# Linear attention layer: head 0's gates and block products ahead of the samples' projection, the samples' state updates behind head 1

## The chip, the cores and the metric

The kernel runs on one core of a Trainium2 chip. The metric is the time of one execution on the device in microseconds, as the median of several runs. The profile is of one execution: its engines are PE (TensorE, matmuls; PEld is its weight load), DVE (VectorE), ACT (ScalarE), POOL (GpSimd) and SP (SyncE, which issues nearly all DMAs here).

## The reference

One inference step of a two-layer decoder: a gated linear attention (GLA) layer, then a differential-attention layer, each followed by an MLP, for one prompt of 16 meta tokens and 1024 tokens and for 8 running sequences ("samples") of one new token each. The change lies wholly in the GLA layer:

```python
def gla_project(x, w_in, w_gate, b_gate):
    h = x @ w_in
    q, k, v, r, g_low = jnp.split(h, [qk, 2 * qk, 2 * qk + vv, 2 * qk + 2 * vv], axis=-1)
    ...
    lg = jax.nn.log_sigmoid((g_low @ w_gate + b_gate).astype(F32)) / GLA_TAU

def gla_chunk(state, q, k, v, lg):
    b = jnp.cumsum(lg, axis=1)
    o_inter = jnp.einsum('blhd,bhde->blhe', q * jnp.exp(b), state)
    causal = jnp.tril(jnp.ones((L, L), bool))[None, :, :, None, None]
    diff = b[:, :, None] - b[:, None, :]
    decay = jnp.where(causal, jnp.exp(jnp.where(causal, diff, 0.0)), 0.0)
    scores = jnp.einsum('bihd,bjhd,bijhd->bhij', q, k, decay)
    o_intra = jnp.einsum('bhij,bjhe->bihe', scores, v)
    b_last = b[:, -1]
    new_state = jnp.exp(b_last)[..., None] * state + jnp.einsum(
        'blhd,blhe->bhde', k * jnp.exp(b_last[:, None] - b), v)
    return new_state, o_inter + o_intra

def gla_sample(x, state, w_in, w_gate, b_gate, g_norm, w_out):
    q, k, v, lg, r = gla_project(x, w_in, w_gate, b_gate)
    s_new, o = gla_chunk(state.astype(F32), q, k, v, lg)
    return gla_output(o, r, g_norm, w_out, x.dtype), s_new
```

There are 4 heads; a head's state is 128 x 256 floats, so one sample's state is 512 KB. The updated states of the samples (`gla_state_s`) and the prompt's final states (`gla_state_p`) are outputs.

## The kernel before

The kernel is one long function; a scheduler orders each engine's instructions by the order in which they are emitted and by its own estimate of when operands are ready. On the chip each engine then runs its list in that fixed order, and a waiting instruction holds up those behind it on its engine. Tiles come from pools; a tile waits until the former holder of its buffer has been read for the last time.

Two streams of work share the GLA layer.

The **prompt** goes head by head, h = 0 to 3. `proj(h, qk)` loads and splits a head's weights into a high and a low part (`unit`, `kunit`; two buffers `whi`/`wlo` each) and projects q and k (2 halves c of 512 tokens, 4 PSUM tiles of pool `mm`, which has 3 banks) and then v (4 more tiles, copied by ACT into `Yh[:, h]`, a part of the big tile Y; L323). Then, for each half c: the gate product (L631), the log gate (L383 to L388), four scans (L639), seven levels of decayed block products (`level`, L420 to L426, on DVE and ACT; L649, L664 on PE), qh (q with decay), kt (k with decay, transposed; L684). Then four steps, each over 128 tokens, advance the state (L692 to L696): three products, one DVE instruction for the new state, which the next step needs. After the four heads come the r gates (kunit, L718 to L727), and then the layer's output projection.

The **samples**, with the meta tokens as 32 rows together, go through the layer's projection (L351, L358), their own gates, their products with the 8 states (L483), their state updates (L484 to L487), the output projection, norm and MLP (L519, L573), and the second layer's projection (L590, L519). Their weights, 48 loads of 1 MB after the states, come through the pool `swt` of two buffers, in the order of emission. The emission of `proj(0)` is interleaved with the samples' projection by `next(first)`; the rest of head 0 and heads 1 to 3 is emitted behind the whole samples' path (L624 and following).

The samples' states pass through three slots in Y. Y holds 8192 columns, head h's v in columns 2048 h to 2048 h + 2047, so that the slots at 5120, 6144 and 7168 lie in the second half of head 2's v and in head 3's v. `sv`, the samples' v, lies in 4096 to 5119. Sample b's slot is loaded, used by the products of L483, multiplied and added to in place with a broadcast of `vs` (in a swt tile, `vbs`), stored, and loaded anew with sample b + 3.

Of the kernel before, what the change touches and what calls it, by code (L numbers as in the profile page):

```python
# [21 lines left out]
P = 128  # L22
# [3 lines left out]
NM = 16  # L26
# [85 lines left out]
def hybrid_step(ctx, tc, A, dbg=None, upto=9):  # L112
# [154 lines left out]
    dma(graw, wir[:, :, 3072:3088])  # L267
    for c in range(2):
# [65 lines left out]
    for c in range(2):  # L334
# [6 lines left out]
        V.tensor_tensor(go, go, ga, op=ALU.add)  # L341
    qk = {}
    first = proj(0, qk)
    next(first)
# [3 lines left out]
    for k in range(NB):  # L348
# [3 lines left out]
        if k % 2:  # L352
            next(first)
    for k in range(0, NB, 2):
# [21 lines left out]
    wg = gp.tile([48, 512], F32, name="wg")  # L376
    for c in range(2):
        dma(wg[32 * c : 32 * c + 16, :], A["gla_w_gate"][0])

    def log_gate(z, n, h):  # L380

        a = t2()[:, :n]
        S.activation(a, z, AF.Abs, bias=bg[:, h : h + 1])  # L383
        S.activation(a, a, AF.Exp, scale=-1.0)
        S.activation(a, a, AF.Ln, bias=1.0)
        m = t2()[:, :n]
        V.tensor_scalar(m, z, bg[:, h : h + 1], 0.0, ALU.add, ALU.min)
        V.tensor_tensor(m, m, a, op=ALU.subtract)  # L388
        return m

# [24 lines left out]
    def level(b, q, k, u, s, eng):  # L415

        sh = [P, b.shape[1] // (2 * s), 2 * s]
        bv = b.rearrange("p (n s) -> p n s", s=2 * s)
        uv = u.rearrange("p (n s) -> p n s", s=2 * s)
        V.tensor_tensor(uv, bv, bv[:, :, s - 1 : s].broadcast_to(sh), op=ALU.subtract)  # L420
        S.activation(uv[:, :, :s], uv[:, :, :s], AF.Exp, scale=-1.0 / 16)
        S.activation(uv[:, :, s:], uv[:, :, s:], AF.Exp, scale=1.0 / 16)
        kv = k.rearrange("p (n s) -> p n s", s=2 * s)
        qv = q.rearrange("p (n s) -> p n s", s=2 * s)
        eng.tensor_tensor(uv[:, :, :s], uv[:, :, :s], kv[:, :, :s], op=ALU.mult)
        eng.tensor_tensor(uv[:, :, s:], uv[:, :, s:], qv[:, :, s:], op=ALU.mult)  # L426


# [18 lines left out]


# [26 lines left out]
    vbs = swt()  # L475
    for b in range(NS):
        stt = Y[:, 5120 + 1024 * (b % 3) : 6144 + 1024 * (b % 3)].rearrange("p (h e) -> p h e", e=256)
        vb = vbs[:, b % 2, :].rearrange("p (h e) -> p h e", e=256)
        with tc.issue_after(w_in):
            dma(stt, A["state_gla"][0, b].rearrange("h d e -> d h e"))  # L480
        dma(vb.rearrange("p h e -> p (h e)"), A["vs"][b : b + 1, :].broadcast_to([P, D]))
        for h in range(GH):
            TE.matmul(po[h * TS : (h + 1) * TS, :256], qmk[:, h, b, :], stt[:, h, :], start=False, stop=b == NS - 1)  # L483
        G.tensor_tensor(vb, vb, bc(skT[:, :, NM + b], [P, GH, 256], 2), op=ALU.mult)  # L484
        for h in range(GH):
            V.scalar_tensor_tensor(stt[:, h, :], stt[:, h, :], ses[:, h, b : b + 1], vb[:, h, :], ALU.mult, ALU.add)
        dma(A["gla_state_s"][0, b].rearrange("h d e -> d h e"), stt)  # L487

    def rstd_of(ssum, n, scale, pool):

        r = pool.tile([P, 8], F32, name="rstd")
        V.tensor_scalar(r[: ssum.shape[0], :n], ssum, scale, EPS, ALU.mult, ALU.add)
        G.tensor_tensor(r[: ssum.shape[0], :n], r[: ssum.shape[0], :n], mhalf[: ssum.shape[0], :n], op=ALU.pow)
        return r[: ssum.shape[0], :n]
# [1101 lines left out]
```

## Time and profile before

| | |
|---|---|
| runs | 2851.33, 2861.34, 2858.92 us; median 2858.92 |
| profiled execution | 2854.81 us, span 2853.1 us, mean granted PE clock 0.989 |
| PE, DVE, ACT, POOL busy | 2741.4, 1950.0, 1094.0, 1112.0 us |
| PE busy in the stretch 100 to 215 us | 92.4 of 115 us |
| first large GLA projection matmul to last r gate | about 33 to 517 us |

A row of the view by stage gives, for a stretch of the span, the busy time of each engine, the granted clock of PE as a share of full speed, the busy share of the DMA engines and their GB/s. A row of the view by tile gives shortest, median and longest duration in ns and the first and last start in us. In rows of groups, the number behind the bar is the total busy time, then the mean in ns, then the idle time of the engine just before, and what ended it. A chain row is a start, a length and what the end of the program was waiting on.

### The profile page before, as it was taken

The page shows a single profiled execution, that of the slowest core. Times are in us where ns is not written, and L with a number is a line of the kernel's source. Part 1 is how long each engine was busy: PE and PEld are TensorE (multiplying, and loading weights), DVE is VectorE, ACT ScalarE, POOL GpSimd, SP SyncE. Part 2 cuts the span into 40 slices and gives each one's busy share as a digit, 9 for nine tenths or more (in the row PEclk, how much of TensorE's full clock was granted, in tenths as well). Part 3 has the DMA queues.
Part 4 walks back from the last instruction along what each step waited for, and adds up shares of the span by engine and source line. Part 5 has one row for each costly group of instructions (what it writes and reads, how often), then busy time and mean ns, then how long its engine had stood idle before and what let it go on. Part 6 is the DMA issues. An engine that isn't in the chain of part 4 may idle for free.

```text
span 2853.1 us, 52265 instructions
## 1 busy us (share of the span) xinstructions
PE 2741.4 (96%) x19849; PEld 2241.7 (79%) x19849; DVE 1950.0 (68%) x3046; ACT 1094.0 (38%) x2229; POOL 1112.0 (39%) x744
## 2 busy tenths in 40 slices
PE   8889999999999999999999999998999999999997
PEld 5666677997777777777799988777888889797985
DVE  2565454668888777777667731888538887878788
ACT  3233344242221321221242112777615546355553
POOL 1221212233343443434234321000326767777764
PEclk9899999999999999999999999999999999999998
DMA  7557741634798898988648994111334455554574
GB/s 255 176 174 260 266 171 39 233 103 154 264 338 308 308 353 300 359 293 322 255 161 321 355 375 133 39 53 49 113 105 89 112 129 116 135 123 115 129 190 89
DMA packets 271833, 560.71 MB, mean 197 GB/s; under 512 B 23559, under 2 KB 138829, under 8 KB 267485
## 3 DMA queue, kind: packets, MB, share of 16 engines
q1 hardware_dynamic: 252284, 520.66, 52.2%
q0 software_dynamic: 19296, 36.71, 7.8%
q8 instruction: 156, 2.56, 0.4%
q14 instruction: 97, 0.79, 0.1%
HBM read 531.16 MB, written 29.26 MB: 196 GB/s over the span
## 4 chain that ended last, share of the span: by engine, by line
PE 74%; DVE 8%; DMA 6%; issue 5%; ACT 4%; POOL 2%; SPq 0%; DVEq 0%; POOLq 0%; ACTq 0%
PE mmt L199 18%; PE mmt L200 17%; PE mmt L201 17%; PE smt L843 4%; PE axt L199 3%; PE axt L200 3%; PE axt L201 3%; ACT as L1190 2%; PE smt L1212 2%; PE prt L1186 1%; PE smt L519 1%; DVE pg L802 1%; DMA swt<-in_mlp_w 1%; PE axt L1207 1%; DMA pg<-in_cache_k 1%
## 5 line engine op out<-in xcount | busy, mean ns | idle before, releaser
L187 POOL TENSOR_TENSOR wlo<-raw,whi 128x512 fp32r<-128x512 f32 x256 | 369.4, 1456 | 770.7 <-ACT whi L186 714.7
L199 PE MATMUL mmt<-whi,XH 128*128 128x256 f32 (+1 forms) x1760 | 523.3, 300 | 2.5 <-ACT Y L323 2.0
L200 PE MATMUL mmt<-wlo,XH 128*128 128x256 f32 (+1 forms) x1760 | 524.1, 299 | 1.5 <-POOL wlo L187 1.5
L199 PE MATMUL mmt<-XH,whi 128*128 128x512 f32 (+1 forms) x1216 | 435.2, 358 | 5.0 <-DVE Y L913 3.0
L201 PE MATMUL mmt<-whi,XL 128*128 128x256 f32 x1536 | 435.1, 285 | 0.0
L201 PE MATMUL mmt<-XH,wlo 128*128 128x512 f32 (+1 forms) x1216 | 431.4, 355 | 0.0
L186 ACT CAST whi<-raw 128x512 fp32r<-128x512 f32 x256 | 152.8, 620 | 593.9 <-PE mmt L201 201.4
L803 DVE TENSOR_REDUCE sc<-pg 128x16 f32<-128x1024 f32 x256 | 308.4, 1211 | 71.5 <-POOL pg L802 69.0
L200 PEld LDWEIGHTS mmt<-wlo,XH 128*128 128x128 f32 x1760 | 331.9, 189 | 28.9 <-issue 16.4
L199 PEld LDWEIGHTS mmt<-whi,XH 128*128 128x128 f32 x1760 | 330.2, 189 | 28.5 <-issue 13.5
L200 PE MATMUL mmt<-XL,whi 128*128 128x512 f32 x768 | 306.2, 399 | 0.0
L802 DVE TENSOR_TENSOR pg<-pg,qb 128x1024 f32<-128x1024 f32 x192 | 258.0, 1351 | 63.0 <-DMA pg<-in_cache_k 56.9
L201 PEld LDWEIGHTS mmt<-whi,XL 128*128 128x128 f32 x1536 | 289.3, 189 | 8.8 <-issue 8.0
L199 PEld LDWEIGHTS mmt<-XH,whi 128*128 128x128 f32 x1216 | 229.1, 189 | 52.2 <-issue 12.9
L802 POOL TENSOR_TENSOR pg<-pg,qb 128x1024 f32<-128x1024 f32 x64 | 165.3, 2584 | 260.8 <-DMA pg<-in_cache_k 198.1
L201 PEld LDWEIGHTS mmt<-XH,wlo 128*128 128x128 f32 x1216 | 229.1, 188 | 34.5 <-issue 1.7
L199 PE MATMUL mmt<-whi,HH 128*128 128x512 f32 x512 | 205.4, 402 | 5.0 <-DVE Y L1027 4.7
L201 PE MATMUL mmt<-whi,HL 128*128 128x512 f32 x512 | 204.5, 399 | 0.0
L200 PE MATMUL mmt<-wlo,HH 128*128 128x512 f32 x512 | 204.0, 398 | 0.0
L1441 POOL TENSOR_TENSOR wlo<-RW,whi 128x512 fp32r<-128x512 f32 x96 | 172.3, 1827 | 47.8 <-ACT whi L1440 47.6
L1441 POOL TENSOR_TENSOR wlo<-rw,whi 128x512 fp32r<-128x512 f32 x92 | 157.4, 1747 | 82.3 <-ACT whi L1440 70.1
L200 PEld LDWEIGHTS mmt<-XL,whi 128*128 128x128 f32 x768 | 145.0, 189 | 38.3 <-issue 7.1
(424 smaller groups left out, 5706.2 us busy)
## 6 DMA issues: line engine op xcount, KB each, us to landing
pg<-in_cache_k SPq DMA_DIRECT2D x256, 512.0 KB, 5.8
pg<-in_cache_v SPq DMA_DIRECT2D x256, 512.0 KB, 6.3
raw<-in_mlp_w SPq DMA_DIRECT2D x164, 256.0 KB, 3.7
swt<-in_mlp_w SPq DMA_DIRECT2D x32, 1024.0 KB, 5.1
rw<-in_mlp_w SPq DMA_DIRECT2D x116, 256.0 KB, 3.4
RW<-in_mlp_w POOLq DMA_DIRECT2D x96, 256.0 KB, 5.7
raw<-in_gla_w_in SPq DMA_DIRECT2D x48, 256.0 KB, 3.5
swt<-in_gla_w_in SPq DMA_DIRECT2D x12, 1024.0 KB, 4.9
```

The costliest lines, as they stand in the source:

```text
L186: S.copy(hi[:, c], raw)
L187: G.tensor_tensor(lo[:, c], raw, hi[:, c].bitcast(F32), op=ALU.subtract)
L199: TE.matmul(ps, ah, bh, start=first, stop=False)
L200: TE.matmul(ps, ah, bl, start=False, stop=False)
L201: return TE.matmul(ps, al, bh, start=False, stop=last)
L519: TE.matmul(ps[o : o + TS, :], lhs[:, k + i, :], t[:, i, c * 512 : (c + 1) * 512], start=k == 0, stop=k == nk - 2)
L802: eng.tensor_tensor(pg, pg, qb, op=ALU.mult)
L803: return V.tensor_reduce(sc[:, n, :], pg.rearrange("p (h d) -> p h d", d=64), op=ALU.add, axis=AX.X).ins
L843: m = TE.matmul(acc[i * TS : i * TS + 16, :256], w[r, n, :], pg[r, i * 256 : (i + 1) * 256], start=n == 0, stop=n == NPG).ins
L1190: S.activation(sc_[:, m, :W], sc_[:, m, :W], AF.Exp, bias=mns[:, m : m + 1], scale=-1.0, accum_out=l[:, m : m + 1])
L1212: TE.matmul(out, at, v, start=j == 0, stop=j == t + 1)
L1441: G.tensor_tensor(lo[:, k, :], t, hi[:, k, :].bitcast(F32), op=ALU.subtract)
```

## The change

It moves code and changes the samples' states; no large matmul is added or removed.

- The steps of a head become functions: `gate_in`, `decays` (gates, blocks, qh, kt), `advance`, `head_end`.
- `decays` of head 0's two halves is emitted inside the samples' projection: the first half ahead of it, the second half after its fourth load. `wg`, the gate weights, is loaded earlier for this. The qh and kt of both halves are kept in Y[:, 2048:4096], head 1's v.
- `advance` of head 0 is emitted right after the meta tokens' state SM, ahead of the samples' own products.
- The samples' states go through five slots, the three in Y and two in a new tile `st2`. All eight samples' products are emitted first, without updates; samples 5 to 7 are loaded into slots 0 to 2 after the products of samples 0 to 2.
- `state_updates` is emitted after head 1: samples 5, 6, 7, 3, 4 out of the slots where they still lie, then 0, 1, 2, loaded a second time into slots 3, 4, 3.

```diff
+    def early(c):
+        o = 2048 + 1024 * c
+        parts.append(decays(0, c, gate_in(0, c), (Y[:, o : o + 512], Y[:, o + 512 : o + 1024])))
+
+    for _ in range(2):
+        next(first)
+    early(0)
...
         if k % 2:
             next(first)
+        if k == 3:
+            early(1)
...
+    st = SM[:, 0, :]
+    for c in range(2):
+        st = advance(0, c, st, *parts[c])
+    head_end(0, st)
...
-    vbs = swt()
+    st2 = spool.tile([P, 2, 1024], F32, name="st2")
+
+    def slot(i):
+        t = Y[:, 5120 + 1024 * i : 6144 + 1024 * i] if i < 3 else st2[:, i - 3, :]
+        return t.rearrange("p (h e) -> p h e", e=256)
...
     for b in range(NS):
-        stt = Y[:, 5120 + 1024 * (b % 3) : 6144 + 1024 * (b % 3)].rearrange("p (h e) -> p h e", e=256)
-        vb = vbs[:, b % 2, :].rearrange("p (h e) -> p h e", e=256)
-        with tc.issue_after(w_in):
-            dma(stt, A["state_gla"][0, b].rearrange("h d e -> d h e"))
-        dma(vb.rearrange("p h e -> p (h e)"), A["vs"][b : b + 1, :].broadcast_to([P, D]))
+        state_in(b, b % 5)
         for h in range(GH):
-            TE.matmul(po[h * TS : (h + 1) * TS, :256], qmk[:, h, b, :], stt[:, h, :], start=False, stop=b == NS - 1)
-        G.tensor_tensor(vb, vb, bc(skT[:, :, NM + b], [P, GH, 256], 2), op=ALU.mult)
-        for h in range(GH):
-            V.scalar_tensor_tensor(stt[:, h, :], stt[:, h, :], ses[:, h, b : b + 1], vb[:, h, :], ALU.mult, ALU.add)
-        dma(A["gla_state_s"][0, b].rearrange("h d e -> d h e"), stt)
...
+            TE.matmul(po[h * TS : (h + 1) * TS, :256], qmk[:, h, b, :], slot(b % 5)[:, h, :], start=False, stop=b == NS - 1)
+
+    def state_updates():
+
+        vbs = swt()
+        for n, (b, i) in enumerate(((5, 0), (6, 1), (7, 2), (3, 3), (4, 4), (0, 3), (1, 4), (2, 3))):
+            stt = slot(i)
+            if b < 3:
+                state_in(b, i)
+            vb = vbs[:, n % 2, :].rearrange("p (h e) -> p h e", e=256)
+            dma(vb.rearrange("p h e -> p (h e)"), A["vs"][b : b + 1, :].broadcast_to([P, D]))
+            G.tensor_tensor(vb, vb, bc(skT[:, :, NM + b], [P, GH, 256], 2), op=ALU.mult)
+            for h in range(GH):
+                V.scalar_tensor_tensor(stt[:, h, :], stt[:, h, :], ses[:, h, b : b + 1], vb[:, h, :], ALU.mult, ALU.add)
+            dma(A["gla_state_s"][0, b].rearrange("h d e -> d h e"), stt)
...
+    for h in range(1, GH):
+        for _ in proj(h, qk):
+            pass
         st = SM[:, h, :]
...
+            st = advance(h, c, st, *decays(h, c, pgs[c]))
+        head_end(h, st)
+        if h == 1:
+            state_updates()
```

Three places show how this moves the instructions. In the rows, a name is the tile written, then an arrow, then what is read; the numbers tell tiles of one name apart.

The first is PE in the kernel before, where the samples' state products start. L454 to L474 are the samples' own block products, L483 the state products, L664 and L649 the blocks of head 0's first half, L199 the q and k projection of head 1:

```order
L454 MATMUL smt_854<-sqk_785 32x32 x4
L463 MATMUL smt_866<-t2_860 32x32 x4
L463 MATMUL smt_878<-t2_872 32x32 x4
L463 MATMUL smt_890<-t2_884 32x32 x4
L463 MATMUL smt_902<-t2_896 32x32 x4
L474 MATMUL smt_913<-Y_87,sA_852 32x256 x4
L483 MATMUL smt_913<-Y_87,s4_910 32x256 x12
L664 MATMUL axt_1476<-t2_1470 32x64 x8
L664 MATMUL axt_1492<-t2_1486 32x32 x8
L649 MATMUL axt_1509<-t2_1503 32x32 x16
```

Now head 0's blocks (L403; L438 is the transpose of kq) stand on PE inside the samples' projection (L484), ahead of head 0's v projection (mmt_912):

```order
L201 MATMUL mmt_669<-XH1_84,wlo_136 128x512
L484 MATMUL smt_616<-swt_900,sx_109 32x512
L403 MATMUL axt_508<-t2_502 32x32 x16
L403 MATMUL axt_532<-t2_526 32x32 x16
L403 MATMUL axt_556<-t2_550 32x32 x16
L403 MATMUL axt_580<-t2_574 32x32 x16
L438 MATMUL axt_608<-c_ident_80,t2_604 128x128 x4
L484 MATMUL smt_616<-swt_900,sx_109 32x512 x3
L484 MATMUL smt_616<-swt_906,sx_109 32x512 x4
L199 MATMUL mmt_912<-whi_157,XH0_83 128x256
```

The blocks of the first half have moved ahead of the samples' sixth load, and the state products have lost their interleaving with them.

The second place is PE after the last product with the samples' second MLP weight. Before, the samples' norm (L542 is its first mean, L528 the transposes ahead of it) has prompt work around it: steps of head 2's advance (L693, L694), blocks of its second half (L664), and head 3's v (mmt_3760):

```order
L542 MATMUL smt_1318<-ss1_1316,c_inv_762 128x32
L693 MATMUL axt_3317<-gS_3313,t2_3277 128x256
L694 MATMUL axt_3317<-Y_87,t2_3289 128x256
L664 MATMUL axt_3362<-t2_3356 32x64 x8
L664 MATMUL axt_3378<-t2_3372 32x32 x8
L199 MATMUL mmt_3760<-whi_3692,XH0_83 128x256
```

Now, with the names left without numbers so that equal rows are counted together; the first L638 is the last MLP product, L647 to L667 the norm, L709 and the second L638 the second layer's projection (8 and 4 loads), L451 to L453 the first step of head 2's second half:

```order
L638 MATMUL smt<-swt,s_1512 32x512 x4
L647 MATMUL smt<-c_ident,s_1726 128x128 x4
L661 MATMUL smt<-ss_1738,c_inv 128x32
L667 MATMUL smt<-ss_1738,c_inv 128x32
L709 MATMUL smt<-swt,sx 32x512 x32
L638 MATMUL smt<-swt,sx 32x512 x16
L451 MATMUL axt<-Y,At_112 128x256
L452 MATMUL axt<-gS,t_3513 128x256
L453 MATMUL axt<-Y,t_3525 128x256
```

The samples' norm and the whole second-layer projection follow one another on PE with no prompt matmul between them.

The third place is DVE, between head 2's second half and head 3. Before, the four steps of the advance (L696) are followed at once by head 3's log gate (L387, L388), scans (L639) and levels (L420):

```order
L696 SCALAR_TENSOR_TENSOR gS_3533<-gS_3321,geb_3527,axt_3529 128x256
L696 SCALAR_TENSOR_TENSOR gS_3541<-gS_3533,geb_3527,axt_3537 128x256
L696 SCALAR_TENSOR_TENSOR gS_3549<-gS_3541,geb_3527,axt_3545 128x256
L696 SCALAR_TENSOR_TENSOR gS_3557<-gS_3549,geb_3527,axt_3553 128x256
L492 TENSOR_SCALAR rstd_3562<-gss_1434 128x8
L387 TENSOR_SCALAR t2_3918<-axt_3910,bg_305 128x512
L388 TENSOR_TENSOR t2_3918<-t2_3918,t2_3914 128x512
```

Now the samples' updates (L612; the first three stand just ahead of the first step, which is now L455 gS_3533) are between them, and L361 is the log gate's last instruction:

```order
L612 SCALAR_TENSOR_TENSOR st2_1396<-st2_1396,ses_1386,swt_2681 128x256 x4
L455 SCALAR_TENSOR_TENSOR gS_3541<-gS_3533,geb_3527,axt_3537 128x256
L612 SCALAR_TENSOR_TENSOR st2_1396<-st2_1396,ses_1386,swt_2681 128x256 x4
L455 SCALAR_TENSOR_TENSOR gS_3549<-gS_3541,geb_3527,axt_3545 128x256
L612 SCALAR_TENSOR_TENSOR st2_1396<-st2_1396,ses_1386,swt_2681 128x256 x4
L455 SCALAR_TENSOR_TENSOR gS_3557<-gS_3549,geb_3527,axt_3553 128x256
L349 TENSOR_SCALAR rstd_3562<-gss_357 128x8
L612 SCALAR_TENSOR_TENSOR st2_1396<-st2_1396,ses_1386,swt_2681 128x256 x4
L406 TENSOR_TENSOR gAd_3926<-axt_3927,c_diag_295 128x128
L360 TENSOR_SCALAR t2_3918<-axt_3910,bg_308 128x512
L612 SCALAR_TENSOR_TENSOR st2_1396<-st2_1396,ses_1386,swt_2681 128x256 x4
L361 TENSOR_TENSOR t2_3918<-t2_3918,t2_3914 128x512
```

All eight updates have moved from the stretch before the samples' output projection to here, and head 3's log gate stands behind the last of them.

More of the change, by code (lines that the diff above doesn't have):

```diff
@@ L267, in hybrid_step @@
     dma(graw, wir[:, :, 3072:3088])
+    wg = gp.tile([48, 512], F32, name="wg")
+    for c in range(2):
+        dma(wg[32 * c : 32 * c + 16, :], A["gla_w_gate"][0])
     for c in range(2):
@@ L375, in hybrid_step @@
     srope = cload("srope", gp)
[L376 to L389, printed above, removed]
     ps = smt()
@@ L446, in hybrid_step @@
         S.copy(SM[:, 2 * hh : 2 * hh + 2, :].rearrange("p h e -> p (h e)"), ps)
+    st = SM[:, 0, :]
+    for c in range(2):
+        st = advance(0, c, st, *parts[c])
+    head_end(0, st)
     sA = spool.tile([TS, GH, TS], F32, name="sA")
```

199 lines of the change are left out of this document (107 added, 92 removed).

## The prediction

> **What bounds the kernel now.** I read the page first, for the engine that sets the end:
>
> ```profile
> span 2853.1 us, 52265 instructions
> PE 2741.4 (96%) x19849; PEld 2241.7 (79%) x19849; DVE 1950.0 (68%) x3046; ACT 1094.0 (38%) x2229; POOL 1112.0 (39%) x744
> PE 74%; DVE 8%; DMA 6%; issue 5%; ACT 4%; POOL 2%; SPq 0%; DVEq 0%; POOLq 0%; ACTq 0%
> ```
>
> TensorE (PE) is busy for 96% and carries 74% of the chain that ended last. The change leaves every large matmul as it is, so its worth is a balance: PE idle time and slow clock removed, against idle time added. The second view was therefore the table by stage. The edited layer runs until about 517 us.
>
> ```profile
> 0.00:100.00 100.00, 89.71 (x608) 65.51 (x609) 22.11 (x44) 27.92 (x50) 22.94 (x21) 1.00 0.75 255
> 100.00:215.00 115.00, 92.36 (x981) 70.43 (x980) 80.85 (x185) 41.62 (x119) 28.42 (x18) 0.88 0.47 155
> 215.00:350.00 135.00, 125.96 (x1352) 87.69 (x1351) 66.31 (x140) 49.47 (x127) 25.63 (x15) 0.99 0.75 263
> 350.00:525.00 175.00, 170.08 (x1548) 134.24 (x1547) 89.88 (x184) 85.09 (x183) 38.35 (x25) 1.00 0.31 103
> ```
>
> The columns are the stretch, its length, the busy time of PE, PEld, DVE (VectorE), ACT and POOL, the granted PE clock, and DMA. From 100 to 215 us PE idles 115 - 92.4 = 22.6 us, and at clock 0.88 its 92.4 busy us contain about 0.12 x 92.4 = 11 us of slow clock. From 215 to 350 it idles 9.0 us, from 350 to 525 only 4.9. In the first 100 us DVE is nearly free (22.1) while PE is full after its start. So there is something to win: 22.6 + 11 + 9.0 = 43 us in all, and DVE room in which to win it. The chief waits of PE between 100 and 350 us:
>
> ```profile
> PE smt L483 <- DMA Y<-in_state_gla: 8.5, 4, 3.4
> PE axt L664 <- DVE t L426: 7.6, 2, 5.6
> PE smt L573 <- DMA swt<-in_mlp_w: 2.8, 4, 0.9
> PE smt L519 <- DMA swt<-in_mlp_w: 3.0, 2, 2.1
> ```
>
> The first is the samples' products waiting for a state whose slot is still being updated, the second head 0's blocks waiting for DVE. Both are among the things that the change moves. The third view was when the samples' path runs, by its PSUM tile smt:
>
> ```profile
> L573 PE MATMUL smt<-swt,sx x128: 592/592/617, 212.3 to 277.0; 128*32 128x512 f32 x128
> L519 PE MATMUL smt<-swt,s x128: 592/596/1057, 282.3 to 348.6; 128*32 128x512 f32 x128
> L483 PE MATMUL smt<-Y,s x64: 379/634/637, 117.6 to 157.0; 128*32 128x256 f32 x64
> L590 PE MATMUL smt<-swt,sx x64: 592/593/617, 371.6 to 403.4; 128*32 128x512 f32 x64
> L519 PE MATMUL smt<-swt,soT x32: 592/592/617, 176.0 to 188.6; 128*32 128x512 f32 x32
> L519 PE MATMUL smt<-swt,sx x32: 592/593/617, 404.6 to 419.1; 128*32 128x512 f32 x32
> ```
>
> State products at 117.6, output projection at 176.0, both MLP weights until 348.6, the second layer's projection (eight loads, then four) until 419.1. All of it has prompt work of heads 1 to 3 beside it.
>
> **Part 1, head 0 early.** Its gates and blocks move from the stretch 90 to 215 us to 45 to 100 us. A half costs DVE, from its groups:
>
> ```profile
> L420 DVE TENSOR_TENSOR t<-gb 128x512 f32<-128x512 f32 x56 | 44.5, 839 | 11.5 <-PE axt L693 7.0 <-PE axt L664 4.2
> L425 DVE TENSOR_TENSOR t<-t,gk 128x256 f32<-128x256 f32 x56 | 27.6, 492 | 0.5 <-ACT t L421 0.4
> L426 DVE TENSOR_TENSOR t<-t,gq 128x256 f32<-128x256 f32 x56 | 23.3, 416 | 0.0
> L639 DVE TENSOR_TENSOR_SCAN gb<-ones,t 128x128 f32<-128x128 f32 x32 | 20.1, 689 | 0.2
> ```
>
> Seven levels of 0.84 + 0.49 + 0.42 are 12.3 us, four scans 2.8, and some 6 for gate, masks and the last two products (estimate): 21 us a half. PE has beside one half 48 projection matmuls; they follow one another every 0.23 us at 512 columns and every 0.12 at 256 (the second half has some 90 of these, again 11 us):
>
> ```profile
> 505.21 0.40 PE L199 MATMUL mmt<-XH,whi 128*128 128x512 f32 x1
> 505.44 0.39 PE L200 MATMUL mmt<-XL,whi 128*128 128x512 f32 x1
> 61.22 0.28 PE L200 MATMUL mmt<-wlo,XH 128*128 128x256 f32 x1
> 61.34 0.28 PE L201 MATMUL mmt<-whi,XL 128*128 128x256 f32 x1
> 45.25 1.07 PE L351 MATMUL smt<-swt,sx 128*32 128x512 f32 x8
> ```
>
> That is 11 us, with 3.5 us of sample products (1.07 us a load) and 3 of blocks: 17.5 of the 21 are covered and PE waits about 4 us in each half, 8 in both. The order has four block groups and a transpose in a row there, with no projection matmul among them. Moved with it, the two wg loads pass ahead of the small loads on SP's queue: nothing, since the first 100 us cover them; uncovered, half a microsecond each.
>
> **Part 2, products before updates.** The products no longer wait for updates, stores and vs broadcasts. Five slots are loaded at once; only samples 5 to 7 wait for a slot that products free. I leave 3 us of the 8.5. Head 0's advance follows directly and fills PE. Waits for MLP weights (2.8 + 3.0) stay: 5.8. Remaining idle is 8 + 3 + 5.8 = 17 of the 43, so **26 us are saved**, with bounds of 14 (DVE chains uncovered, 30 left) and 38 (5 left). Head 1's v copies now wait until head 0's qh and kt in that part of Y are read; PSUM banks cover this, without them some 5 us.
>
> **Part 3, the updates late.** They are emitted behind head 1, but their broadcast tile is a swt tile, and swt hands out two buffers in the order of emission, behind all the samples' weights. So the first update starts after the second layer's 11th load has been used. Until its store lands, slot 0 lies in Y[:, 5120:6144], which is head 2's v for its second half. Its two PSUM tiles cannot be copied out; head 3's first v tile needs slot 1. These three are all the banks of mm. The order fits: from the last MLP product on, PE has 12 loads' products and the norm in a row and no prompt work. That stretch is serial. Its prices:
>
> ```profile
> 352.81 0.68 DVE L525 COPY s<-smt 128x512 f32<-128x512 f32 x1
> 368.93 0.43 DVE L561 TENSOR_TENSOR sx<-sz,lnp 128x256 f32<-128x256 f32 x1
> 222.95 20.75 SPq L227 DMA_DIRECT2D swt<-in_mlp_w x6
> swt<-in_mlp_w SPq DMA_DIRECT2D x32, 1024.0 KB, 5.1
> swt<-vs SPq DMA_DIRECT2D x8, 512.0 KB, 6.1
> 129.66 1.92 POOL L484 TENSOR_TENSOR swt<-swt,sqk 128x1024 f32<-128x1024 f32 x1 [28.14 <-DMA swt<-vs]
> 149.12 1.67 DVE L486 SCALAR_TENSOR_TENSOR Y<-Y,ses,swt 128x256 f32<-128x256 f32 x4 [4.33 <-POOL swt L484]
> 135.38 3.47 DMA out_gla_state_s<-Y
> 139.33 6.46 DMA out_gla_state_s<-Y
> ```
>
> The norm ran from 348.6 to 369.4, 20.8 us, with DVE shared; its 17 DVE instructions alone are about 6 us, with PE, ACT and hand-overs 10 (estimate): I take 10, since DVE is then empty. Weights: two loads are ahead; a buffer turns over in 5.1 (landing) + 1.07 (product) + 0.6 (issue and signals, estimate) = 6.8 us, and the 11th load is five turns and a product later: 35 us. Six loads issued over 20.75 us give 3.5 to 4.2 each, which fits. Then vs 6.1, POOL 1.9, DVE 1.7, store 4.5 (between 3.5 and 6.5), copy and signals 1: 15. Sum 10 + 35 + 15 = 60 us, less PE's own work in it (12 x 1.07 + 1 = 14): **46 us of PE idle added**. Bounds: 37, with nine loads at the fastest rate seen (below), and 66, with the norm at 20.8 and twelve loads in 47.5 as before.
>
> ```profile
> 180.00:185.00 5.00, 3.32 (x135) 2.24 (x135) 3.85 (x10) 3.52 (x8) 0.00 (x0) 1.00 1.01 371
> ```
>
> At 371 GB/s a 1 MB load takes 2.8 us, nine take 25. The Trainium skill, "DMA: Bandwidth & Descriptors", section Specifications, puts HBM's limit for a core near 358 GB/s; by it nine loads would take 26 us and the sum fall by 8. The window of 371 differs slightly, and the measurement decides.
>
> **Part 4, after the stretch.** On DVE the updates stand between the steps of head 2's second half, and all eight ahead of head 3's log gate; they come one broadcast apart, the last three also one store and one state load. Updates to the eighth take about 48 us from the first broadcast (8 at 4 to 8 us, estimate from the rows above). PE meanwhile has head 3's v and the first r gates, 144 x 0.117 + 56 x 0.23 = 30 us: I take 8 us of waits, 3 of clock recovery (estimate, from the 0.50 rows below), less the 5 idle that stood there: **+6** (0 to 16).
>
> **Sum.** -26 + 46 + 6 = +26. The profiled execution took 2854.8 (span 2853.1 and 1.7 around it), so 2880.8; the median of the runs is 4.1 above that, 2858.9, and on it the forecast is **2885 us**. The next stage starts when this one's pools close and PE is 97% busy there, so nothing absorbs the delay:
>
> ```profile
> 525.00:2853.00 2328.00, 2263.30 (x15368) 1883.79 (x15366) 1690.83 (x2497) 889.92 (x1752) 996.66 (x668) 0.99 0.62 199
> ```
>
> **Rivals.** *Half clock in the stretch.* While PE was sparsely busy, its clock was halved:
>
> ```profile
> 125.00:130.00 5.00, 2.73 (x96) 2.40 (x96) 5.00 (x15) 2.26 (x7) 0.34 (x1) 0.50 1.03 280
> 130.00:135.00 5.00, 1.73 (x40) 0.72 (x40) 5.00 (x6) 0.67 (x3) 3.57 (x2) 0.50 0.89 323
> 135.00:140.00 5.00, 3.53 (x76) 2.71 (x77) 5.00 (x14) 1.32 (x3) 0.00 (x0) 0.50 0.71 212
> ```
>
> A load's product would then take up to 1.9 us (1057 against 592 ns in the smt rows), once per buffer turn: 6 x 0.85 = 5, and 3 more to recover: +34, 2893. Chance 0.17. The Trainium skill, "TensorE: Matmul & The Clock Gate", Part 1, says the array falls to half clock after an idle window of about 3.4 us and returns after as long of steady work. That rule speaks for this rival, and the 0.50 rows agree with it.
>
> *Head 3 becomes the bound.* Its gates start only after the eighth update, near 92 us after the last MLP product; if its DVE chain, two halves and eight steps, stretches as it does today between other work, PE waits for it ahead of the last r gates: 20 us more, +46, 2905. For: three PSUM banks again. Against: r gates give PE cover. Chance 0.14.
>
> *No change.* The loads run at 2.8 us (stretch 51, idle 37), the front saves 38: about 0, 2859. Within 0.3%, 8.6 us, a measurement of this kernel can't tell it from no change. Chance 0.12.
>
> *Faster.* The stretch is as short as that, and the front and the tail of the layer lose all their idle: -43 + 37 - 5 = -11, 2848. For: DVE is free where the work goes, and the stores and broadcasts leave the samples' weights alone. Against: the DVE chain of 21 us under 17.5 of cover. It decides where the serial stretch falls below what the front saves plus PE's 14 us. Chance 0.08.
>
> **How the numbers follow.** The forecast itself, +9 to +40, has 0.49. Slower is 0.49 + 0.17 + 0.14 = 0.80, same 0.12, faster 0.08. The range reaches from +4 (38 saved, 37 added, 5 after) to +50 (26 saved, 60 added, 16 after): 2863 to 2909. It leaves out the faster case, half of no change and the upper third of head 3's.
>
> **What would show it.** Right: between 100 and 215 us PE busy near 105 and clock near 1.00; near 340 us a stretch of some 60 us with PE about a quarter busy and only smt products; head 2's second-half steps starting after the first state store; end of the layer near 545 us. Wrong: prompt matmuls inside that stretch, a stretch under 45 us, or PE idle in the front as before.

## The result and the profile after

The changed kernel takes 2901.88 us (median of 4 runs, 2895.86 to 2907.11), the kernel before 2858.45 in the same comparison: ratio 1.0149, 95% interval 1.0127 to 1.0171, some 43 us slower. The forecast was 2885 (+26), the range to 2909. The profiled execution took 2907.11, at the upper end of its runs.

The page, and the table by stage (columns as in the prediction):

```profile
span 2905.4 us, 52280 instructions
PE 2766.6 (95%) x19849; PEld 2249.9 (77%) x19849; DVE 1940.9 (67%) x3046; ACT 1098.2 (38%) x2233; POOL 1101.3 (38%) x744
```

```profile
0.00:100.00 100.00, 87.49 (x904) 61.63 (x905) 49.61 (x115) 42.64 (x90) 16.05 (x16) 0.95 0.60 202
100.00:215.00 115.00, 113.07 (x946) 87.33 (x946) 38.29 (x110) 34.03 (x99) 21.48 (x15) 0.99 0.39 131
215.00:350.00 135.00, 120.55 (x1358) 81.73 (x1356) 62.89 (x144) 49.87 (x131) 21.20 (x14) 0.96 0.76 262
350.00:525.00 175.00, 135.12 (x1044) 94.88 (x1045) 71.42 (x145) 59.95 (x125) 38.14 (x22) 0.80 0.45 148
```

From 100 to 215 us PE (TensorE) now idles 115 - 113.1 = 1.9 us instead of 22.6: that part of the change does what it says. From 350 to 525 it idles 39.9 instead of 4.9, and the clock is 0.80 instead of 1.00. From 215 to 350, which the forecast expected to gain too, the idle time grew from 9.0 to 14.5. The waits of PE up to 575 us name what stands there:

```profile
PE smt L709 <- DMA swt<-in_diff_w_in: 11.8, 6, 3.4
PE axt L451 <- ACT Y L327: 9.5, 1, 9.5
PE smt L638 <- DMA swt<-in_diff_w_in: 6.6, 4, 2.4
PE smt L638 <- DMA swt<-in_mlp_w: 5.1, 5, 1.6
PE axt L418 <- DVE t L375: 4.1, 3, 1.6
PE smt L692 <- DMA swt<-in_mlp_w: 2.8, 2, 2.6
```

L709 and L638 with `in_diff_w_in` are the second layer's projection, L692 and L638 with `in_mlp_w` are the products with the two MLP weights, L418 is a group of a head's blocks. L451 is the first step of head 2's second half, and L327 is the copy of head 2's v out of PSUM. What ACT waited for ahead of that copy, from ACT's own waits:

```profile
ACT Y L327 <- DMA out_gla_state_s<-Y: 11.1, 2, 7.6
```

It waited for the store of the state that lies in head 2's place. The chain of waits in order of time (start, length, what) shows the whole stretch between:

```profile
347.05 1.11 PE smt L638 x8
348.19 0.70 DVE s L644
...
354.56 3.10 issue
357.66 3.68 PE smt L709 x16
361.36 7.10 DMA swt<-in_diff_w_in
368.50 1.98 PE smt L709 x8
370.49 5.30 DMA swt<-in_diff_w_in
375.83 1.98 PE smt L709 x8
377.83 4.94 DMA swt<-in_diff_w_in
382.81 1.98 PE smt L709 x8
384.81 5.03 DMA swt<-in_diff_w_in
389.88 1.98 PE smt L638 x8
391.87 5.22 DMA swt<-in_diff_w_in
397.14 1.98 PE smt L638 x8
...
401.00 3.22 DVE Y L612 x4
```

After the last MLP product (347.05) comes the norm up to 357.7, then twelve loads in two buffers that take turns of landing and product (some 7.2 us for one landing and the product behind it, 9.1 in the first turn), then the first update (L612) at 401.0; L451 starts at 408.6 (its row stands beside those of an experiment below). A load's eight products take 1.98 us in it, not 1.07. And PE's clock in two windows of 5 us within the stretch and two behind it:

```profile
365.00:370.00 5.00, 3.14 (x16) 0.20 (x8) 0.00 (x0) 0.00 (x0) 0.00 (x0) 0.50 0.84 313
395.00:400.00 5.00, 1.94 (x8) 0.20 (x8) 0.00 (x0) 0.83 (x2) 1.01 (x1) 0.50 0.80 307
410.00:415.00 5.00, 5.00 (x21) 4.49 (x20) 2.06 (x5) 1.29 (x4) 3.00 (x2) 0.58 0.63 238
415.00:420.00 5.00, 5.00 (x40) 4.85 (x39) 2.16 (x5) 0.90 (x4) 1.48 (x2) 1.00 0.89 291
```

The samples' path, and the last instructions of the layer (before at 519.6, by the second row), by their groups:

```profile
L599 PE MATMUL smt<-Y,s x48: 378/379/404, 151.0 to 163.0; 128*32 128x256 f32 x48
L638 PE MATMUL smt<-swt,soT x32: 592/593/617, 172.2 to 183.1; 128*32 128x512 f32 x32
L638 PE MATMUL smt<-swt,s x128: 592/616/1062, 282.6 to 347.5; 128*32 128x512 f32 x128
L774 DVE SCALAR_TENSOR_TENSOR Y<-axt,gn,swt x16: 742/745/751, 525.7 to 562.6; 128x512 f32<-128x512 f32 x16
```

```profile
L727 DVE SCALAR_TENSOR_TENSOR Y<-axt,gn,swt x16: 740/746/754, 482.7 to 519.6; 128x512 f32<-128x512 f32 x16
```

The layer ends 562.6 - 519.6 = 43.0 us later. From there to the end of the span are 2342.8 us here and 2333.5 before. Over all the profiles of this study that rest lay between 2333.5 and 2349.3, and the kernel before is the lowest of them, so the other 9 us are no more than executions differ by.

### The profile page after: what moved, and what is told of

Same layout as the page of the kernel before. It is cut to its first block, busy times and chain, and to the rows that moved or that the text cites. A ratio compares the mean times of both kernels' runs of the same rounds, so it can differ in the third digit from the quotient of the medians.

```text
span 2905.4 us, 52280 instructions
## 1 busy us (share of the span) xinstructions
PE 2766.6 (95%) x19849; PEld 2249.9 (77%) x19849; DVE 1940.9 (67%) x3046; ACT 1098.2 (38%) x2233; POOL 1101.3 (38%) x744
## 4 chain that ended last, share of the span: by engine, by line
PE 74%; DVE 10%; DMA 6%; ACT 4%; issue 4%; POOL 1%; SPq 0%; DVEq 0%; POOLq 0%; ACTq 0%
PE mmt L199 17%; PE mmt L200 17%; PE mmt L201 17%; PE smt L890 4%; PE axt L199 3%; PE axt L200 3%; PE axt L201 3%; ACT as L1237 2%; PE smt L1259 2%; PE smt L638 1%; DVE pg L849 1%; DVE RX L1463 1%; DMA swt<-in_diff_w_in 1%; PE prt L1233 1%; DMA swt<-in_mlp_w 1%
## 5 line engine op out<-in xcount | busy, mean ns | idle before, releaser
L187 POOL TENSOR_TENSOR wlo<-raw,whi 128x512 fp32r<-128x512 f32 x256 | 363.3, 1433 | 802.2 <-ACT whi L186 707.7
L199 PE MATMUL mmt<-whi,XH 128*128 128x256 f32 (+1 forms) x1760 | 525.0, 301 | 0.8 <-ACT gk L314 0.5
L199 PE MATMUL mmt<-XH,whi 128*128 128x512 f32 (+1 forms) x1216 | 437.1, 360 | 8.0 <-DVE HL L196 3.8
L199 PEld LDWEIGHTS mmt<-whi,XH 128*128 128x128 f32 x1760 | 331.2, 189 | 34.5 <-issue 21.0
L849 DVE TENSOR_TENSOR pg<-pg,qb 128x1024 f32<-128x1024 f32 x192 | 266.0, 1393 | 67.1 <-DMA pg<-in_cache_k 54.9
L199 PEld LDWEIGHTS mmt<-XH,whi 128*128 128x128 f32 x1216 | 231.2, 190 | 51.6 <-issue 7.6
L199 PE MATMUL mmt<-whi,HH 128*128 128x512 f32 x512 | 205.4, 402 | 5.1 <-DVE Y L1074 5.0
```

The source lines that it names most:

```text
L187: G.tensor_tensor(lo[:, c], raw, hi[:, c].bitcast(F32), op=ALU.subtract)
L199: TE.matmul(ps, ah, bh, start=first, stop=False)
L849: eng.tensor_tensor(pg, pg, qb, op=ALU.mult)
```

## The experiments

Every ratio is against the kernel before, run on the same chip in the same comparison (its medians were 2853.3 to 2858.5). The balance behind each expectation is PE's idle time plus its slow clock (busy time times the missing share of the clock), summed over windows of 5 us, as idle/slow in us:

| kernel | ratio (95%) | 0-100 | 100-215 | 215-350 | 350-525 | last row of the layer, us |
|---|---|---|---|---|---|---|
| before | 1 | 10.3/0 | 22.6/8.9 | 9.0/1.6 | 4.9/0 | 519.6 |
| after | 1.0149 (1.0127-1.0171) | 12.5/3.7 | 1.9/1.5 | 14.5/4.3 | 39.9/17.8 | 562.6 |
| e1 | 0.9985 (0.9971-0.9998) | 12.2/2.6 | 1.9/1.4 | 18.2/3.9 | 7.6/1.3 | 513.1 |
| e2 | 1.0046 (1.0032-1.0060) | 11.7/2.8 | 7.3/1.4 | 5.2/1.5 | 21.9/12.7 | 530.7 |
| e3 | 1.0110 (1.0095-1.0125) | 10.2/0 | 7.8/5.4 | 10.6/6.0 | 33.8/13.1 | 548.6 |
| e4 | 0.9971 (0.9961-0.9982) | 11.0/1.2 | 7.7/2.2 | 6.7/1.3 | 9.6/1.6 | 506.6 |
| e5 | 0.9951 (0.9934-0.9967) | 10.8/0 | 14.5/8.2 | 2.4/0 | 3.9/1.1 | 502.2 |
| e6 | 0.9971 (0.9959-0.9983) | 12.6/2.2 | 6.4/1.4 | 4.8/1.4 | 12.0/4.7 | 512.6 |
| e7 | 0.9988 (0.9977-0.9999) | 9.3/1.5 | 8.1/2.9 | 18.6/2.5 | 4.1/0 | 507.8 |
| e8 | 0.9984 (0.9972-0.9996) | 13.2/1.3 | 5.9/2.7 | 9.2/1.5 | 8.1/1.6 | 509.4 |
| e9 | 0.9966 (0.9954-0.9979) | 12.2/2.4 | 1.1/0 | 5.0/0 | 13.1/2.4 | 500.4 |
| e10 | 1.0182 (1.0161-1.0204) | 12.5/1.5 | 1.9/0 | 18.8/2.3 | 26.9/7.7 | 560.0 |
| e11 | 1.0132 (1.0116-1.0147) | 13.6/2.3 | 1.7/0 | 17.5/4.6 | 36.7/16.2 | 554.8 |
| e12 | 0.9982 (0.9971-0.9993) | 12.1/2.7 | 10.7/4.2 | 6.7/1.6 | 7.3/2.6 | 510.3 |

### The parts, one at a time

**e1: the broadcasts out of the weights' buffers.**

```
-        vbs = swt()
...
+            for e in range(2):
+                vb = t2()
+                v2 = vb.rearrange("p (h e) -> p h e", e=256)
+                dma(vb, A["vs"][b : b + 1, e * 512 : e * 512 + 512].broadcast_to([P, 512]))
```

> The late updates stay behind head 1, but their vs broadcasts land in the small t tiles (512 columns, two per sample) and no longer in a buffer of the samples' weights. Theory (the loss is the serial stretch, because the broadcast tile stands behind all the samples' weights): the stretch of 60 us without prompt matmuls is gone, L451 of head 2's second half no longer waits for a store, the clock stays near 1.00 from 350 to 420 us, and the front's gain remains: 2838 to 2846 us, 12 to 20 below before. Rival 1 (the samples' weights on two buffers set the end, whatever else is done): the gain of the front comes back as idle time beside the second layer's loads, 2855 to 2862. Rival 2 (the updates on VectorE ahead of head 2's gates are the cost): over 2870.

2852.49 us, ratio 0.9985. The stretch is gone, and prompt work stands beside all the loads again. That the broadcasts wait behind the samples' weights is thus one condition of the loss. The time is between the theory's and the first rival's: of the gain between 100 and 215 us, 28 us, 11.5 are given back between 215 and 350. The updates now share the DMA with the MLP weights there: PE's longest wait, and the window (DMA share 0.91 against 0.75 before):

```profile
PE smt L640 <- DMA swt<-in_mlp_w: 10.7, 5, 4.5
```

```profile
215.00:350.00 135.00, 116.85 (x1323) 81.12 (x1324) 83.06 (x162) 49.12 (x131) 39.07 (x30) 0.95 0.91 313
```

The MLP products last from 211.2 to 361.8 us, 151 us against 135 in the changed kernel. How much of the loss is the shared DMA isn't shown, since the changed kernel lost nearly as much in this window without it (18.8 us of idle and slow clock, 22.1 here).

**e2: head 0 early, alone.** As the changed kernel, with the loop over the samples' states of before in its old place.

```
     for b in range(NS):
-        state_in(b, b % 5)
...
+        G.tensor_tensor(vb, vb, bc(skT[:, :, NM + b], [P, GH, 256], 2), op=ALU.mult)
...
-        if h == 1:
-            state_updates()
```

> Head 0 early alone; the samples' states are read and updated one by one with three slots as before the change. Theory: the front's idle and slow clock between 100 and 215 us fall by some 15 to 20 us of the 31 (the wait of the products for updated slots stays), nothing else changes: 2838 to 2848. Rival 1 (the samples' weights set the end): PE idles as much more beside the second layer's loads, 2855 to 2862. Rival 3 (it is head 0's move that costs): over 2870.

2867.58 us, ratio 1.0046: slower than before, at a price between those of the two rivals. The front gained (31.5 us of idle and slow clock became 8.7) and the end of the layer lost 29.7. The samples' rows show why: state products, output projection, last four loads.

```profile
L594 PE MATMUL smt<-Y,s x64: 379/379/404, 148.9 to 183.1; 128*32 128x256 f32 x64
L623 PE MATMUL smt<-swt,soT x32: 592/617/1063, 203.0 to 215.3; 128*32 128x512 f32 x32
L623 PE MATMUL smt<-swt,sx x32: 592/1061/1064, 438.2 to 455.2; 128*32 128x512 f32 x32
```

Against 117.6, 176.0 and 404.6 before: head 0's work, put ahead, delays the samples' chain by 31, 27 and 34 us. PE is full in the front, and in its order the samples' small steps stand behind prompt products. At the end the prompt runs out of work while the loads come.

**e3: products first and updates late, head 0 where it was.**

In the kernel before, the samples' part is the changed kernel's from `st2` to `state_updates`, and in the loop over the heads:

```
         G.tensor_tensor(Yh[:, h], Yh[:, h], bc(rr, [P, 8, 256], 2), op=ALU.mult)
+        if h == 1:
+            state_updates()
```

> The products first and the updates behind head 1, in the same buffer of the samples' weights, with head 0 where it was before the change. Theory: the serial stretch is there too, but since head 0's work comes later only the last 8 of the 12 loads stand bare in PE's order: some 30 to 35 us of idle and slow clock instead of 53, less about 6 of state waits in the front: 2880 to 2892. Rival 3 (head 0's move is the cost): 2850 to 2862.

2887.16 us, ratio 1.0110, as the theory had it. The same wait stands in front of head 2's second half (first row), and the output projection starts at 142.2 us instead of 176.0 (last row):

```profile
PE axt L707 <- ACT Y L323: 9.9, 1, 9.9
PE smt L605 <- DMA swt<-in_diff_w_in: 8.1, 4, 3.9
```

```profile
L534 PE MATMUL smt<-swt,soT x32: 592/592/617, 142.2 to 154.2; 128*32 128x512 f32 x32
```

So products first takes 34 us out of the samples' chain. The two parts alone cost 0.46% and 1.10%, together 1.49%: the sum agrees. That doesn't show that the changed kernel holds the same two losses, since e2's came from a late samples' chain (e6 below), and in the changed kernel the chain isn't late.

**e5: products first, updates right behind them, head 0 where it was.** As e3, with the call moved:

```
-        if h == 1:
-            state_updates()
...
+    state_updates()
+
     so = spool.tile([P, 256], F32, name="so")
```

> The state products first, the updates right behind them (broadcasts in a buffer of the samples' weights, ahead of the output projection), and head 0 where it was before the change. Theory from the runs so far (idle and slow clock of TensorE up to 525 us add up to the time; 57 us before): 10 at the start, 13 between 100 and 215 us as with the late updates alone, 7 at the output projection, 8 and 5 behind it, 44 in all: 2840 to 2848. Rival (products first is worth something only with head 0 early): 2854 to 2862.

2843.30 us, ratio 0.9951, as the theory had it: 0.5% below before and 2% below the changed kernel. It is the lowest ratio of all, though its interval overlaps those of e4, e6 and e9. The order of products and updates is useful by itself, without head 0 early.

**e4: the same with head 0 early**, that is, the diff of e5 on the changed kernel.

> As the changed kernel, but the updates are emitted right behind the state products, ahead of the samples' output projection; the broadcast tile then stands ahead of the samples' later weights. Theory: no serial stretch, 2836 to 2848, though the output projection's first load waits for the eight broadcasts (up to 25 us later than 172). Rival 1 (the samples' weights set the end): the later chain costs what the front gains or more, 2855 to 2868.

2846.12 us, ratio 0.9971, as the theory had it. Its interval overlaps e5's: head 0 early adds nothing to it that these runs show.

**e7: late updates with broadcasts in t tiles, head 0 where it was**, the diff of e1 on e3.

> Products first and updates behind head 1 with the broadcasts in t tiles, head 0 where it was before the change. Theory: the front's 23 us of idle and slow clock up to 215 us as with the late updates alone, no serial stretch, some 18 us beside the MLP weights (the broadcasts, state loads and stores share the DMA with them), 5 behind: 46 against 57, 2844 to 2852. Rival (late updates cost even with a buffer of their own): 2860 to 2875.

2851.23 us, ratio 0.9988, as the theory had it, with the same idle beside the MLP weights as e1 (18.6 us).

### What holds back whom

**e9: the three states in Y updated right behind the products**, the other five where the changed kernel has them, with the broadcast tile still behind the samples' weights.

```
+    for b, i in ((5, 0), (6, 1), (7, 2)):
+        stt = slot(i)
+        for e in range(2):
+            vb = t2()
...
-        for n, (b, i) in enumerate(((5, 0), (6, 1), (7, 2), (3, 3), (4, 4), (0, 3), (1, 4), (2, 3))):
+        for n, (b, i) in enumerate(((3, 3), (4, 4), (0, 3), (1, 4), (2, 3))):
```

> As the changed kernel, but the three states in Y (samples 5 to 7) are updated right behind the products, with broadcasts in t tiles; the other five stay behind head 1, their broadcast tile behind all the samples' weights. Theory (the stretch comes from head 2's and head 3's v, which find their place in Y taken; late updates elsewhere hold nobody): no stretch, L451 doesn't wait for ACT, 2845 to 2856. Rival (the late updates themselves, on VectorE between head 2's and head 3's steps, hold up PE): 2870 or more.

2847.90 us, ratio 0.9966, as the theory had it. Five updates are as late as ever and hold up PE little: one wait of 3.9 us at 426.9, for block copies on DVE (L426) that stand behind an update which itself waited 4.5 us for its reloaded state. Their row, and the window from 215 to 350 us:

```profile
L624 DVE SCALAR_TENSOR_TENSOR st<-st,ses,swt x20: 471/476/2183, 408.5 to 436.3; 128x256 f32<-128x256 f32 x20
```

```profile
215.00:350.00 135.00, 130.00 (x1458) 92.63 (x1457) 67.41 (x149) 50.87 (x140) 20.71 (x14) 1.00 0.77 264
```

The three slots in Y alone are worth 1.0149 - 0.9966 = 1.8% or 52 us. The second row adds a point that the prediction lacked: with them free, PE idles 5.0 us between 215 and 350 instead of 14.5. So the prompt had begun to starve ahead of the last MLP product. The projections' PSUM tile mmt in that window, of the changed kernel and of this one (PE's busy time on it, clock, DMA share):

```profile
215.00:350.00 135.00, 61.56 (x342) 0.96 0.76 262
```

```profile
215.00:350.00 135.00, 73.23 (x420) 1.00 0.77 264
```

Some 12 us of prompt projection are missing there. The table says the same of all kernels: the six that update the states in Y behind head 1 (the changed kernel, e1, e3, e7, e10, e11) lose 16.6 to 22.1 us of idle and slow clock between 215 and 350, the eight others 2.4 to 10.7.

**e6: head 0 early alone (e2), with the r gates' Silu in t tiles.**

```
-        silt = swt().rearrange("p k (c n) -> p k c n", c=2)
...
-                s_ = silt[:, m, c, :]
+                s_ = t2()
```

> As head 0 early alone (2867.6), but the Silu of the r gates goes to small t tiles and no longer to a tile of the samples' weights' buffers. Theory: the r gates may start only when the samples' 11th load of the second layer has been used, and head 0 early makes the samples late (output projection from 203 us instead of 176), so that TensorE runs out of prompt work; with the r gates free of that buffer they fill the 35 us of idle and slow clock between 350 and 525 us: 2838 to 2848. Rival (the r gates wait for head 3 or for PSUM, not for the samples): 2862 to 2872.

2846.47 us against 2867.58, ratios 0.9971 and 1.0046: the theory held. The r gates' Silu tiles are the same kind of buffer as the samples' weights, and the first one is freed by the 11th load. First and last Silu in e2 and here:

```profile
L750 ACT ACTIVATE swt<-mmt x16: 587/597/605, 447.3 to 530.1; 128x512 f32<-128x512 f32 x16
```

```profile
L749 ACT ACTIVATE t<-mmt x16: 588/597/605, 413.2 to 512.0; 128x512 f32<-128x512 f32 x16
```

In e2 the 11th load's products end at 447.25 us, and the first Silu starts at 447.3. So a late samples' chain also delays the r gates, and that is what made head 0 early alone lose. The same two lines in the kernel before were not run; it idles only 4.9 us between 350 and 525, so they could win little there.

**e8: the same two lines in e4.**

> As the changed kernel with the updates right behind the products (2846.1), and the Silu of the r gates in t tiles. Theory: only 11 us of idle and slow clock stand between 350 and 525 us there, of which the r gates can fill about half: 2840 to 2846. Rival (the r gates are not held back there): 2846, no difference.

2850.84 us, ratio 0.9984 (e4 0.9971): no gain, so the rival's time, but not its reason. The r gates are held back in e4 too, though little: the first Silu comes at 423.9 us, where the 11th load's products end at 423.5, and at 418.7 in e8. Those 5 us, against 34 between e2 and e6, brought nothing.

### Two that did not go as expected

**e10: the stretch filled.**

```
-    pa = smt()
+    pa, pd = smt(), smt()
...
+        for i in range(6):
+            TE.matmul(pd[:, :256], ident, sx.rearrange("p k t -> p (k t)"), start=True, stop=True)
```

> As the changed kernel, with 48 more products (ident against sx, 128x256, result unused) between the first eight loads' products of the second layer, where TensorE otherwise waits: they only keep it busy. Theory: a load's product falls back from 1.98 to about 1.07 us, and since each turn of two buffers holds one such product besides the landing, three or four turns get 0.9 us shorter: stretch 56 to 58 instead of 60.5 us, 2896 to 2900 us. Rival a (half clock is worth the 15 us of slow clock that the balance shows there): 2885 to 2890. Rival b (the landing alone sets the turn, the added products only take time): 2902 to 2910.

2909.04 us, ratio 1.0182 (the changed kernel 1.0149, intervals overlapping). The clock came back to 0.94 while the fillers ran, and the median product of a load to 617 ns from 1061. But PE was then full (31.7 of 32 us), and the first eight loads took longer. The window of e10, and the loads' groups there and in the changed kernel:

```profile
348.00:380.00 32.00, 31.70 (x160) 19.56 (x160) 0.13 (x1) 0.00 (x0) 0.00 (x0) 0.94 0.61 204
```

```profile
L709 PE MATMUL smt<-swt,sx x64: 592/617/1062, 348.2 to 379.6; 128*32 128x512 f32 x64
```

```profile
L709 PE MATMUL smt<-swt,sx x64: 1034/1061/1063, 357.7 to 383.7; 128*32 128x512 f32 x64
```

31.4 us instead of 26.0: the filler was too much and became the bound itself. The time is rival b's, but not for its reason, since not the landing but PE set the turn. The run shows that a busy PE brings the clock back, and nothing of what half clock costs. That price stays open.

**e11: head 0's advance behind the samples' products.** 

```
-    st = SM[:, 0, :]
-    for c in range(2):
-        st = advance(0, c, st, *parts[c])
-    head_end(0, st)
...
         for h in range(GH):
             TE.matmul(po[h * TS : (h + 1) * TS, :256], qmk[:, h, b, :], slot(b % 5)[:, h, :], start=False, stop=b == NS - 1)
+    st = SM[:, 0, :]
...
+    head_end(0, st)
```

> As the changed kernel, but head 0's state steps (advance and its end) are emitted behind the samples' state products and no longer ahead of them. Theory (the samples' chain sets where the stretch begins, and head 0's early work had put the chain back by some 31 us, which the products-first order only made up for): the state products come about 14 us earlier, near 137 instead of 151, the last MLP product near 334 instead of 347.5, the stretch is as long, the layer ends about 14 us earlier: 2884 to 2892. Rival (the prompt's work, not the samples' chain, sets the end): 2898 to 2906.

2895.92 us, ratio 1.0132. The products started at 147.5 us instead of 151.0, where 137 was expected. So the advance is only a small part of the delay; the rest must lie in the steps ahead of it, in which PE hardly idles (1.7 us from 100 to 215). The stretch begins and ends ten us earlier, L451 first in the changed kernel, then here:

```profile
L451 PE MATMUL axt<-Y,At x8: 377/506/794, 408.6 to 418.1; 128*128 128x256 f32 x8
```

```profile
L451 PE MATMUL axt<-Y,At x8: 378/506/793, 398.7 to 407.1; 128*128 128x256 f32 x8
```

How many of those ten are the edit's isn't shown. In e10, whose PE order ahead of the stretch is that of the changed kernel, the MLP products also end earlier, at 338.6 instead of 347.5, so executions of one order differ by that much: their first one starts at 209.2 instead of 212.7, and they take 129.4 us instead of 134.8. In e11 the ten are there at the first one (202.7), and the products take 135.4. Theory and rival can't be told apart by it.

**e12: the same edit in e4.**

> As e4 (updates right behind the products, 2846), with head 0's state steps behind the products. Theory: the samples' chain 14 us earlier gives the r gates an earlier start, which takes about half of the 11 us of idle and slow clock left between 350 and 525 us: 2838 to 2844. Rival (PE is full there, nothing to win): 2846 or more.

2853.57 us, ratio 0.9982: no gain, and not distinctly slower than e4. The theory fell here: the output projection starts no earlier to any use, since PE waits for its weights, which stand behind the broadcasts (7.0 us in e4, more here):

```profile
PE smt L640 <- DMA swt<-in_gla_w_out: 10.6, 3, 7.6
```

## Why the prediction was right, and where its sum was off

**Part 3, the stretch: right in mechanism and length, in part by luck.** Forecast 60 us as 10 + 35 + 15. Measured, from 348.19 to 408.6: 9.5 to the first load's product, 37 to the issue of the first broadcast at 394.8 (first row below), 14 from there to L451. In the 37 two misses offset each other: products of 1.98 us instead of 1.07 add 0.9 to each of the five turns, and the 0.6 for issue and signals, which no run shows (the gaps in the chain are at most 0.05 us), takes most of it out again.

```profile
L609 SPq DMA_DIRECT2D swt<-vs x8: 349/442/497, 394.8 to 428.5; - x8
L612 DVE SCALAR_TENSOR_TENSOR st<-st,ses,swt x20: 473/481/3826, 415.8 to 441.9; 128x256 f32<-128x256 f32 x20
```

The mechanism has two conditions, the broadcast tile behind the samples' weights and the state in head 2's v; e1 and e9 each take away one and with it the loss. The third link, that three full PSUM banks stop the projections, was only read from the program and the waits: no product on mmt runs between 345.4 and 411.8 us, two copies of v run at 407.9, right behind a store, and the third at 412.6, behind another; no run varied the number of banks. The net price, forecast at 46 of idle time: of the changed kernel's 350-525 column in the table 34.4/14.9 fall between 350 and 420 us, 49.3 in all, against 3.4 before. Idle time alone grew by 31; the rest is slow clock, since PE was busy at half clock for 25.0 of the 60.4 us, two fifths and not the quarter that was forecast.

**Part 4: right in size.** Forecast +6; the rest of that column, behind 420 us, is 5.5/2.9 against 1.5, +6.9.

**Parts 1 and 2, the front: this is the step that failed, a term of the wrong size.** Forecast: 17 of 43 us remain, 26 saved; the 17 are 8 for head 0's two DVE chains, 3 for states and 5.8 for MLP weights. Measured: 3.4 of idle and slow clock between 100 and 215 and 18.8 between 215 and 350, 22.2 of 42.1, so 20 saved; and 5.9 more were lost ahead of 100 us. The net is 14, not 26. With it the sum is -14 + 46 + 7 = +39, against +43 at the layer's end; the other 4 are not accounted for.

Term by term: the 5.8 beside the MLP loads is the one that failed, 18.8 measured. The waits for the MLP weights themselves grew only to 7.9 (5.1 and 2.8, in the first list of waits above); the rest is mostly waits for DVE, and 4.3 of slow clock. The prompt starves not only from the last MLP product on but well ahead of it, and that goes with the borrowed slots (e9: 9.5 us of idle and 4.3 of slow clock between 215 and 350 us go with them). The 8 for the DVE chains did not come: between 35 and 215 us PE waits 0.2 us for DVE in head 0's blocks (the 4.1 in L418's row lie behind 215). Lost instead, at the very start and put at nothing in the forecast, are 2.2 of idle and 3.7 of slow clock between 15 and 35 us, where PE waits for small loads and the first samples' weights (L292 1.6 us, L484 2.0; 0.3 and 0.7 before). All kernels with head 0 early have slow clock ahead of 100 us (1.2 to 3.7, the others 0 to 1.5); whether the two wg loads, now ahead on the queue, cause it was not tested.

One effect is not in the sum at all, and for part 1 alone it turned the gain into a loss: head 0's work ahead of the samples' delays the samples' chain by 31 us up to the state products (e2), and products first takes 34 out again (e3). The two cancel, so that the last MLP product came at 347.5 instead of 348.6, and the prediction's place for the stretch was right by this accident (in e10, with the same order up to there, it came at 338.6). The prediction treated PE's idle time as the only thing to win and the samples' chain as given.

**The rivals.** *Half clock in the stretch* (0.17): this is what happened. From the first load's product to L451 the clock was 0.50, and a load's products took 1.98 us. Its price, 5 us in the turns, is hidden in the sum: a turn took 7.2 us where 6.8 was forecast, 0.4 more instead of 0.9, because of the 0.6 that is not there (landing mostly 4.9 to 5.3, then product). Whether the turns would have been shorter at full clock is open (e10). The 3 us to recover fit: PE was busy from 408.6 without a gap and back at 1.00 from 414.2, so 5.6 us at half clock, a loss of 2.8. The Trainium skill, "TensorE: Matmul & The Clock Gate", Part 1, names a window of about 3.4 us for the fall and the return, and calls it free-running. The return took 5.6 us here, which is between one and two such windows. For the fall no wait of that length was needed: the clock fell at 349.3, when the longest wait of the last 4 us had been 1.6 us, and it stayed at 0.50 with waits of at most 3.4 (the last section). *Head 3 becomes the bound* (0.14): not seen; the last update, ahead of its log gate, began 441.9 - 348.2 = 94 us after the last MLP product, near the forecast's 92 (second row above), and PE had the r gates' projection beside it (idle 5.5 us from 420 to 525). *No change* and *faster* needed a stretch of 51 us or less; it was 60.4. *What would show it*: PE busy near 105 between 100 and 215 (113), the 60 us with smt products only, head 2's steps behind the first store, all seen; PE about a quarter busy was two fifths, at half clock, and the layer's end near 545 was 562.6.

## What to carry to other kernels

A tile from a rotating pool is handed out in the order of emission: work that is emitted late and takes a tile from the pool of another, long stream stands behind the whole of that stream, however early its data are there. If it also holds memory that other work must write to (here a borrowed place in Y), that work stops, and the engine with it; freeing the borrowed place was worth 52 us, and with either condition taken away (e1, e9) the kernel was no slower than before. And before moving work ahead into idle time, follow the second chain through the same engine: in e2 TensorE's gaps were filled as planned (22.8 us of idle and slow clock less between 100 and 215), and the samples' chain came 31 us later, which by way of the r gates' buffer cost 29.7 us behind 350.

## What the runs showed of the hardware

While the first eight loads came, PE was busy for 14.5 of 27 us, more than half of the time, and no wait among these products was over 3.4 us. Yet the clock stood at 0.50 all the while. It had fallen at 349.3: in the 3.4 us before that, PE was busy for 1.43 us, and its longest wait was 1.6. Filled with other products (e10), it came back to 0.94.

```profile
357.00:384.00 27.00, 14.51 (x64) 1.90 (x64) 0.53 (x2) 0.00 (x0) 0.00 (x0) 0.50 0.77 265
```

An update's four VectorE instructions took 3.22 us for the first sample (chain above) and 1.67 for a later one (the one at 412.1); why the first was slower was not tested.
